# Low parts of the gate and up weights: written by an accumulating DMA instead of VectorE

## The chip, the cores and the metric

One core of a Trainium2 chip runs the kernel. The metric is the device time of one execution in microseconds, the median of several runs. The engines are called PE (TensorE, with PEld for its weight loads), DVE (VectorE), ACT (ScalarE), POOL (GpSimd) and SP (SyncE), as the profile calls them.

## The reference

A trunk of two layers on 512 tokens of 1024 features, in float32. Each layer mixes a state-space branch and a windowed attention branch, and ends in a gated feed-forward block of 2816 hidden features, which is where the change lies:

```python
    u = rms_norm(h, norm_ffn[layer])
    gate, up = jnp.split(u @ w_gate_up[layer], 2, axis=-1)
    h = h + (jax.nn.silu(gate) * up) @ w_down[layer]
```

## The kernel before

**Products in three parts.** A weight product is made in the float32r format, which carries fewer bits than float32. So each operand is split into a high part (its value in float32r) and a low part (the rest), and each block of the contraction takes three matmuls: high times high, high times low of the activations, low of the weights times high (`split3`, line 245). In the trace the weights are `hi` and `lo`, the normalised activations `nh` and `nl`, or `uh` and `ul` where the tokens' norm factors are still missing.

**The stream of weights.** All weights pass through one list of chunks, in the order of use (lines 495 to 510). A gate or up chunk (`w_gu`) holds one tile of 128 output features: 128 partitions of 8 x 128 values, 512 KB. Three stages handle it. `w_load` (line 197) has SP's queue load it into one of 3 `raw` buffers. `w_split` (line 221) writes `hi` with ACT, which converts `raw` to float32r, and then `lo` with DVE, which subtracts `hi` from `raw`. `hi` and `lo` have 4 buffers each. `proj` (line 335) runs the 24 matmuls of a tile.

**How far ahead.** `w_ahead` (line 231) splits chunks up to a number and keeps loads up to 3 chunks beyond. `proj` calls it at its start and half-way, so that while chunk c runs, `hi` of chunk c + 3 is written; its buffers are those of chunk c - 1. A `raw` buffer is loaded again once the split has read it.

**The start of gate and up.** `proj_first` (line 368) runs the first three tiles together, a block of the contraction at a time, since the last block of their input comes late. Meanwhile DVE and ACT work out the norm's factors and the normalised input (`Norm.finish`, line 478: `un`, `nh`, `nl`). The fourth tile also takes the input without factors (`NRAW` = 4); DVE multiplies the products of these four by the factors afterwards (`nu`). Tiles 4 to 43 take `nh` and `nl`. Since the first three tiles hold three pairs of buffers until their end, the split of chunk 4 has to wait for the end of the first tiles.

**Evacuation.** A gate tile leaves its PSUM bank `acc` by a tanh on ACT (`ft`) and a product on DVE (`fg`); an up tile by a product on DVE (`fu`), a conversion on ACT (`fh`) and a subtraction on DVE (`fl`), lines 1133 to 1155. These are the inputs of the down products.

**The order.** Each engine carries out its instructions in the order in which the program issues them. That order comes from a rough account of time in the program (`Clock`, line 70): work beside the weight products is issued when by this account its operands are ready (`poll`, line 294). POOL adds and multiplies in the branches and has nothing to do in the feed-forward block. All lines of compute instructions read L66 in the profile, since a helper issues them; loads from SP read L141.

Of the kernel before, what the change touches and what calls it, by code (L numbers as in the profile page):

```python
# [16 lines left out]
T = 512  # L17
# [26 lines left out]

# columns of the packed constants
C_ID, C_TRI, C_ONE, C_M0, C_M12, C_COS, C_SIN = 0, 128, 256, 384, 512, 768, 1280
NRES = 768
NCONST = 1792
# columns of one layer's packed vectors
V_NM, V_NF, V_CW, V_CB, V_DS, V_SN, V_DTB, V_AL = 0, 8, 16, 112, 136, 152, 168, 200  # L50
# [4 lines left out]
class Engine:  # L55
    """Passes an engine's calls on and keeps the time at which it is through with them."""

# [12 lines left out]
class Clock:  # L70
    """A rough account of when each tile is ready, by which the order of issue is chosen: work that
    hangs on other engines is put between the weight products when its operands are there."""

# [59 lines left out]
def trunk_kernel(ctx: ExitStack, tc: tile.TileContext, xT, consts, vecs, w_in, w_v0, w_v, w_ssd, w_attn,  # L133
# [45 lines left out]
    def take(n):  # L179
        """Waits until n of the side work's banks are free, and takes them."""  # L180
        while room[0] < n:
            yield
        room[0] -= n
# [7 lines left out]

# [1 line left out]
    chunks = []  # L193
    raws, parts_, freed = {}, {}, {}
    state = {"load": 0, "split": 0, "use": 0}
# [8 lines left out]
    def w_halves(i, part):  # L204
        """The first chunks by halves of the contraction: loaded (part 0, 1), split (2, 3)."""
        nk, f = chunks[i].shape[1], chunks[i].shape[2]
        s = slice(part % 2 * (nk // 2), (part % 2 + 1) * (nk // 2))
        if part == 0:
            raws[i] = wpool.tile([P, nk, f], F32, tag="raw", bufs=RAW_BUFS, name=f"raw{i}")
        if part < 2:  # L210
            load(raws[i][:, s, :], chunks[i][:, s, :])
            return
        if part == 2:
            parts_[i] = [wpool.tile([P, nk, f], F32R, tag=x, bufs=HL_BUFS, name=f"{x}{i}") for x in ("hi", "lo")]
        hi, lo = parts_[i]
        sca.activation(out=hi[:, s, :], in_=raws[i][:, s, :], func=AF.Copy)
        dve.tensor_tensor(out=lo[:, s, :], in0=raws[i][:, s, :], in1=hi[:, s, :].bitcast(F32), op=ALU.subtract)
        if part == 3:
            del raws[i]

    def w_split(i):
        raw = raws.pop(i)
        nk, f = raw.shape[1], raw.shape[2]
        hi = wpool.tile([P, nk, f], F32R, tag="hi", bufs=HL_BUFS, name=f"hi{i}")
        lo = wpool.tile([P, nk, f], F32R, tag="lo", bufs=HL_BUFS, name=f"lo{i}")
        sca.activation(out=hi, in_=raw, func=AF.Copy)
        dve.tensor_tensor(out=lo, in0=raw, in1=hi.bitcast(F32), op=ALU.subtract)
        parts_[i] = (hi, lo)
        freed[i] = clock.ready[Clock.key(lo)]
# [22 lines left out]

# [1 line left out]
    class Task:  # L254
# [11 lines left out]
    def arrived(t):  # L266
        """Waits for a load."""
        while clock.ready[Clock.key(t)] > clock.now["pe"]:
            yield
# [24 lines left out]
    def poll():  # L294
        """Runs the next stage of whatever has its operands by now."""
        for name in active:
# [27 lines left out]
    def drain(ready):  # L324
        """Runs the side work until ready(): nothing else is left to do before that."""
        while not ready():
            clock.now["pe"] += 0.3
            poll()
# [6 lines left out]
    def proj(act, nk, ev, nchunks=1):  # L335
        """One tile of 128 output features: nk blocks of the contraction, in nchunks chunks."""
        ps = acc_room()
# [12 lines left out]
    def proj_tokens(act, nk, ev, pss, nchunks):  # L350
        """256 or more output features with the tokens on partitions, in two banks or four."""
        uh, ul = act
# [15 lines left out]
    def proj_first(n, evs, at=3):  # L368
        """The first tiles after a norm, from its input that lacks the tokens' factors: a block of the
        contraction at a time, as the last one comes late. The factors are worked out meanwhile."""  # L370
        norm = isinstance(n, Norm)
# [20 lines left out]

# [1 line left out]
    def rsqrt_small(vv, n):  # L394
        """1/sqrt of a small tile, by Newton steps from the exponent's halving."""
        y = small("nr_y", n, 2)
# [10 lines left out]
    def norm_sums(sq, cs=range(4)):  # L407
        """Sums over features of a tile of squares, a column for each 128 tokens."""
        ps = bank()
# [9 lines left out]
    def norm_rows(y):  # L419
        """The tokens' factors as a row, on every partition."""  # L420
        ps = bank()
# [11 lines left out]
    class Norm:  # L433
        """u = h * w, in two parts; the tokens' factors are applied to the products."""

# [35 lines left out]
        def finish(self, fs):  # L471
            """The normalised input in two parts."""
            def low(u, hi, lo):
# [13 lines left out]

# [1 line left out]
    for l in range(DEPTH):  # L489
# [14 lines left out]
        for f in range(KD):  # L504
            chunks.append(w_out[l, f])
        for f in range(2 * KF):
            chunks.append(w_gu[l, f])
        for f in range(KD):
# [30 lines left out]
    for l in range(DEPTH):  # L539
        L = {}  # L540

        def normed(ps, raw):
            """A product, times the tokens' factors if its input lacked them."""
            if not raw:
# [4 lines left out]

        # -- dt, its running sums and decays --  # L550
        def ev_dt(pss):
            """The columns behind the first heads' V: dt's, with tokens on partitions."""
            tmp = slot(nm="dtt")
# [58 lines left out]

        # -- SSD: convolution and gate where the products come out --
        def ev_conv(g, what, ps, raw=False):
# [34 lines left out]
        def ssd_tasks(g, l, L):  # L649
# [6 lines left out]
            def hd(t, c):  # L656
                """A small tile's values of this group's heads in chunk c, for each of 64 columns."""
                return t[:, c * 32 + 8 * g:c * 32 + 8 * g + 8].unsqueeze(2).to_broadcast([P, 8, 64])
# [4 lines left out]
            def prep():  # L663
                """B C^T of each chunk, x dt and B with tokens on partitions, the states between chunks."""
                while "acr" not in L:
# [65 lines left out]
            def decays():  # L731
                """C B^T times exp(a_cum[l] - a_cum[s]), a head at a time."""
                while "acr" not in L:
# [86 lines left out]

        # -- attention --
        def ev_attn(hd, what, ps):
# [17 lines left out]
        def ev_v(hp, pss):  # L840
            """V of two heads with tokens on partitions, and again with tokens 4 j + a in tile a."""
            vn, vp = [slot(nm="vn"), slot(nm="vn")], [slot(nm="vp"), slot(nm="vp")]
# [20 lines left out]
        def attn_chain(hd, l, L):  # L863
# [22 lines left out]

            # pattern 0: tile i's queries on the keys of tiles i - 1 and i, packed as (0, 1), (2, 3)
            yield from take(2)
# [15 lines left out]
            for i in range(4):  # L904
                b, o, n = where[i]
                sca.activation(out=p0[b][:, o:o + n * P], in_=p0[b][:, o:o + n * P], func=AF.Exp,
                               scale=SCALE, bias=nb[:, i:i + 1], accum_out=st[:, 4 + i:5 + i])
            # patterns 1 and 2: tokens 4 j + a of tile a
            yield from take(2)
# [14 lines left out]
            for a in range(4):  # L924
                o = (a % 2) * 256
                sca.activation(out=p1[a // 2][:, o:o + 256], in_=p1[a // 2][:, o:o + 256], func=AF.Exp,
                               scale=SCALE, bias=nb[:, 4 + a:5 + a], accum_out=st[:, 12 + a:13 + a])
            # transposes of pattern 0's weights: block (i, cur) at i, block (i, prev) at i - 1
            yield from take(2)
# [93 lines left out]

        # -- branch outputs, gates --
        def parts_of(x, to):
            """A tile in two parts, at the end of the lists to."""
            hi, lo = slot(F32R, nm="ah"), slot(F32R, nm="al")
# [80 lines left out]

        # -- output projection, residual --
        nf = Norm(v(l, V_NF, 8))  # L1110
# [17 lines left out]

        # -- feed-forward --
        hid = ([], [])  # L1130
# [37 lines left out]

    # -- the last tile by halves of the tokens, the final norm behind each --
    ws = [w_next(0) for _ in range(3)]  # L1170
# [45 lines left out]
def in_order(l):  # L1216
    """The order of a layer's products up to the output projection: columns of the input projection
    ("in"), groups of the SSD branch ("a"), tiles of the attention branch ("b")."""
    def S(g):
# [6 lines left out]
    def mix(*lists):  # L1226
        """The lists' items in turn, each list spread over the whole."""
        n = [(i + 0.5) / len(x) for x in lists for i in range(len(x))]
# [19 lines left out]
def _columns():  # L1248
    """w_in's columns by tile: (z | x | B | C | dt | q | k | v | g_ssd | g_attn) in the kernel's numbering."""
    z0, x0, b0, c0, dt0 = 0, 2048, 4096, 4608, 5120  # L1250
# [89 lines left out]
```

## Time and profile before

| what | value |
|---|---|
| median of 3 runs | 2398.57 us (2398.03 to 2398.86) |
| span of the profiled execution | 2397.4 us |
| PE, DVE, ACT, POOL busy | 2370.2, 1309.6, 982.4, 162.4 us |
| mean granted clock of PE | 0.997 |
| gate and up chunks, in both layers | 88 of 512 KB |
| matmul of 512 columns, mean | 389 ns in the gate and up stage |
| high part of a chunk, ACT | 1.05 us |
| low part of a chunk, DVE | 1.23 us |

The profiled execution's span runs from its first to its last instruction; its own time with what lies around that is not given, so the span is set beside the median of the runs. Matmuls overlap in the pipeline: one takes 389 ns, but they start some 227 ns apart. In a timeline row stand the start, the duration, the engine, the instruction with its output and input, and in brackets the idle time of the engine before it and what ended that.

### The profile page before, as it was taken

The page shows a single profiled execution, that of the slowest core. Times are in us where ns is not written, and L with a number is a line of the kernel's source. Part 1 is how long each engine was busy: PE and PEld are TensorE (multiplying, and loading weights), DVE is VectorE, ACT ScalarE, POOL GpSimd, SP SyncE. Part 2 cuts the span into 40 slices and gives each one's busy share as a digit, 9 for nine tenths or more (in the row PEclk, how much of TensorE's full clock was granted, in tenths as well). Part 3 has the DMA queues.
Part 4 walks back from the last instruction along what each step waited for, and adds up shares of the span by engine and source line. Part 5 has one row for each costly group of instructions (what it writes and reads, how often), then busy time and mean ns, then how long its engine had stood idle before and what let it go on. Part 6 is the DMA issues. An engine that isn't in the chain of part 4 may idle for free.

```text
span 2397.4 us, 30515 instructions
## 1 busy us (share of the span) xinstructions
PE 2370.2 (99%) x11830; PEld 1982.2 (83%) x11830; DVE 1309.6 (55%) x2099; ACT 982.4 (41%) x1697; POOL 162.4 (7%) x132
## 2 busy tenths in 40 slices
PE   8999999999999999999999999999999999999998
PEld 6878888888888888888888887888888888888887
DVE  7566656565555564443375647566545545644333
ACT  5454545554532332222245445364635323322222
POOL 0011111011000000000001101011110000000000
PEclk9999999999999999999999999999999999999999
DMA  4534435343333322233334344353433333322331
GB/s 154 171 91 137 133 92 153 95 147 111 102 104 105 131 97 99 95 99 106 117 112 147 98 144 127 95 151 114 124 104 113 113 105 110 106 97 97 94 98 64
DMA packets 100704, 272.83 MB, mean 114 GB/s; under 512 B 13584, under 2 KB 20368, under 8 KB 100560
## 3 DMA queue, kind: packets, MB, share of 16 engines
q1 hardware_dynamic: 100560, 270.89, 35.6%
q8 instruction: 93, 1.52, 0.3%
q14 instruction: 51, 0.42, 0.1%
HBM read 251.64 MB, written 10.81 MB: 109 GB/s over the span
## 4 chain that ended last, share of the span: by engine, by line
PE 95%; DVE 2%; DMA 1%; ACT 1%; SPq 0%; issue 0%; POOL 0%; DVEq 0%; POOLq 0%
PE acc L66 84%; PE ps L66 10%; DMA R<-acr 1%; DVE lo L66 1%; SPq L141 0%; DVE cacc L66 0%; DVE z L66 0%; DMA h<-xT 0%; DVE h L66 0%; DMA k<-rp 0%; ACT hi L66 0%; DMA raw<-w_in 0%; DVE un L66 0%; ACT uh L66 0%; ACT sq L66 0%
## 5 line engine op out<-in xcount | busy, mean ns | idle before, releaser
L66 PE MATMUL acc<-nh,hi 128*128 128x512 f32 x1984 | 791.3, 399 | 2.1 <-DVE nu L66 2.1
L66 DVE TENSOR_TENSOR lo<-raw,hi 128x1024 fp32r<-128x1024 f32 (+2 forms) x397 | 490.1, 1238 | 536.3 <-ACT hi L66 531.7
L66 PE MATMUL acc<-nh,lo 128*128 128x512 f32 x1984 | 774.0, 390 | 0.0
L66 PE MATMUL acc<-nl,hi 128*128 128x512 f32 x1984 | 773.3, 390 | 0.0
L66 ACT ACTIVATE hi<-raw 128x1024 fp32r<-128x1024 f32 (+2 forms) x397 | 409.0, 1032 | 234.4 <-PE acc L66 133.9
L66 PEld LDWEIGHTS acc<-nh,hi 128*128 128x128 f32 x1984 | 373.3, 188 | 79.0 <-issue 5.9
L66 PEld LDWEIGHTS acc<-nh,lo 128*128 128x128 f32 x1984 | 372.8, 188 | 78.9
L66 PEld LDWEIGHTS acc<-nl,hi 128*128 128x128 f32 x1984 | 373.4, 188 | 77.2 <-issue 3.4
L66 PE MATMUL acc<-ah,hi 128*128 128x512 f32 x384 | 151.0, 393 | 0.0
L66 PE MATMUL acc<-ah,lo 128*128 128x512 f32 x384 | 149.6, 389 | 0.0
L66 PE MATMUL acc<-al,hi 128*128 128x512 f32 x384 | 149.4, 389 | 0.0
L66 PE MATMUL acc<-fh,hi 128*128 128x512 f32 (+1 forms) x374 | 141.1, 377 | 0.5 <-DVE h L66 0.5
L66 PE MATMUL acc<-fl,hi 128*128 128x512 f32 (+1 forms) x374 | 140.8, 376 | 0.0
L66 PE MATMUL acc<-fh,lo 128*128 128x512 f32 (+1 forms) x374 | 140.8, 376 | 0.0
L66 ACT ACTIVATE fh<-fu 128x512 fp32r<-128x512 f32 x44 | 27.8, 632 | 190.2 <-DVE fu L66 190.2
L66 DVE SCALAR_TENSOR_TENSOR cacc<-acc,vec,cacc 128x511 f32<-128x511 f32 (+2 forms) x120 | 89.4, 747 | 16.4 <-ACT cacc L66 13.6
L66 POOL TENSOR_TENSOR rs<-rs,sin 128x512 f32<-128x512 f32 x16 | 27.6, 1728 | 997.0 <-DVE rs L66 997.0
L66 ACT ACTIVATE p<-p,nb 128x256 f32<-128x256 f32 (+1 forms) x128 | 61.8, 484 | 70.2 <-DVE nb L66 70.1
L66 ACT ACTIVATE R<-R,acum 128x128 f32<-128x128 f32 x256 | 81.1, 388 | 16.2 <-DMA R<-acr 16.2
L66 PEld LDWEIGHTS acc<-ah,lo 128*128 128x128 f32 x384 | 72.1, 188 | 15.3
L66 PEld LDWEIGHTS acc<-al,hi 128*128 128x128 f32 x384 | 72.1, 188 | 14.7
L66 PEld LDWEIGHTS acc<-ah,hi 128*128 128x128 f32 x384 | 72.1, 188 | 14.4
(172 smaller groups left out, 2958.2 us busy)
## 6 DMA issues: line engine op xcount, KB each, us to landing
raw<-w_in SPq DMA_DIRECT2D x173, 512.0 KB
raw<-w_gu SPq DMA_DIRECT2D x88, 512.0 KB
R<-acr SPq DMA_DIRECT2D x64, 256.0 KB
raw<-w_ssd SPq DMA_DIRECT2D x32, 512.0 KB
raw<-w_dn SPq DMA_DIRECT2D x32, 512.0 KB
E<-acr SPq DMA_DIRECT2D x64, 128.0 KB
r<-fd SPq DMA_DIRECT2D x32, 256.0 KB
raw<-w_attn SPq DMA_DIRECT2D x16, 512.0 KB
```

The costliest lines, as they stand in the source:

```text
L66: return f(*a, **kw)
```

## The change

For the chunks of the gate and up products from the fifth one of each layer on (40 per layer, 80 in all) the low part is made in another way. ACT writes the high part as before, and then writes into `lo` the chunk once more with its sign turned, converted to float32r in the same way: the negated high part. Then a DMA from POOL's queue reads the chunk from memory a second time and adds it to `lo`. What is left is the chunk less its high part, as before. DVE has no part in it. The `raw` buffer is free when ACT has read it twice. The account of time hears of ACT's second instruction and not of the DMA.

```diff
     chunks = []
+    by_dma = set()
...
         sca.activation(out=hi, in_=raw, func=AF.Copy)
+        if i in by_dma:
+            sca.activation(out=lo, in_=raw, func=AF.Copy, scale=-1.0)
+            freed[i] = clock.ready[Clock.key(lo)]
+            nc.gpsimd.dma_start(lo, chunks[i], accum_op=ALU.add)
+            parts_[i] = (hi, lo)
+            return
         dve.tensor_tensor(out=lo, in0=raw, in1=hi.bitcast(F32), op=ALU.subtract)
         parts_[i] = (hi, lo)
         freed[i] = clock.ready[Clock.key(lo)]
...
         for f in range(2 * KF):
+            if f >= NRAW:
+                by_dma.add(len(chunks))
             chunks.append(w_gu[l, f])
```

The rest of the diff takes comments and docstrings out. PE's and SP's instructions stand in the same order in both kernels. On ACT the 80 new instructions stand right behind the high parts; on DVE the 80 subtractions are gone; POOL gets 80 DMAs in a row of 40 for each layer.

ACT's order before, at the start of gate and up in layer 0. `hi_7263`, `hi_7303` and `hi_7321` are the high parts of chunks 4, 5 and 6; the numbers of tiles differ a little between the two programs.

```order
L66 ACTIVATE nh_7228<-un_7227 128x512
L66 ACTIVATE hi_7263<-raw_7096 128x1024
L66 ACTIVATE ft_7270<-nu_7267 128x512
L66 ACTIVATE ft_7280<-nu_7277 128x512
L66 ACTIVATE nh_7283<-un_7282 128x512
L66 ACTIVATE nh_7288<-un_7287 128x512
L66 ACTIVATE nh_7294<-un_7293 128x512
L66 ACTIVATE hi_7303<-raw_7122 128x1024
L66 ACTIVATE hi_7321<-raw_7261 128x1024
```

The same place after, where chunks 4, 5 and 6 are `hi_7263`, `hi_7304` and `hi_7323`:

```order
L66 ACTIVATE nh_7228<-un_7227 128x512
L66 ACTIVATE hi_7263<-raw_7096 128x1024
L66 ACTIVATE lo_7264<-raw_7096 128x1024
L66 ACTIVATE ft_7271<-nu_7268 128x512
L66 ACTIVATE ft_7281<-nu_7278 128x512
L66 ACTIVATE nh_7284<-un_7283 128x512
L66 ACTIVATE nh_7289<-un_7288 128x512
L66 ACTIVATE nh_7295<-un_7294 128x512
L66 ACTIVATE hi_7304<-raw_7122 128x1024
L66 ACTIVATE lo_7305<-raw_7122 128x1024
L66 ACTIVATE hi_7323<-raw_7261 128x1024
L66 ACTIVATE lo_7324<-raw_7261 128x1024
```

Each negated high part stands right behind its high part, ahead of the evacuation (`ft`) and of the normalised input (`nh`) that followed the high part before.

POOL's order after, at the same place. The first two rows are its last work in the attention branch of layer 0:

```order
L66 TENSOR_TENSOR p_6211<-p_6145 128x256
L66 TENSOR_TENSOR p_6211<-p_6146 128x256
L231 DMA lo_7264<-w_gu 128x1024
L231 DMA lo_7305<-w_gu 128x1024
L231 DMA lo_7324<-w_gu 128x1024
```

Before, POOL's next row there is its first work of layer 1; the 40 DMAs of the layer have come in between, each waiting for its negated high part.

## The prediction

> **What bounds the kernel now.** I read the page first, then who TensorE (PE) waits for, then the chain of waits and the stages of the changed products.
>
> The page of the kernel before:
>
> ```profile
> span 2397.4 us, 30515 instructions
> ...
> PE 2370.2 (99%) x11830; PEld 1982.2 (83%) x11830; DVE 1309.6 (55%) x2099; ACT 982.4 (41%) x1697; POOL 162.4 (7%) x132
> ...
> PEclk9999999999999999999999999999999999999999
> ...
> PE 95%; DVE 2%; DMA 1%; ACT 1%; SPq 0%; issue 0%; POOL 0%; DVEq 0%; POOLq 0%
> ```
>
> PE is busy all the time at full clock and is 95% of the chain that ended last. All that PE waited for between 45 and 2370 us (total, times, longest), and the chain's longest piece in layer 0:
>
> ```profile
> PE ps L66 <- DVE H L66: 3.3, 2, 1.7
> PE ps L66 <- DVE xdt L66: 1.3, 2, 0.9
> PE ps L66 <- ACT tpp L66: 0.6, 1, 0.6
> ```
>
> ```profile
> 850.59 355.01 PE acc L66 x1566
> ```
>
> None of these waits is for a weight chunk. The 355 us piece covers the whole gate and up stage of layer 0 without a gap. The stages themselves (stretch, its length, busy time of PE, PEld, DVE, ACT, POOL, then clock, DMA share, GB/s):
>
> ```profile
> 871.00:1220.00 349.00, 349.00 (x1547) 289.17 (x1546) 145.99 (x176) 101.04 (x129) 0.00 (x0) 1.00 0.31 103
> 2054.00:2270.00 216.00, 216.00 (x955) 178.85 (x954) 93.17 (x106) 64.82 (x84) 0.00 (x0) 1.00 0.29 100
> ```
>
> So DVE is 42% busy there, ACT 29%, POOL idle, the DMA engines 30%: PE alone is full. Time can be lost here, hardly won.
>
> **The change, part by part.** *Removed:* 80 subtractions on DVE. *Added:* 80 negations on ACT, 80 DMAs from POOL's queue. PE's and SP's orders stay as they were, row for row. In the steady stage the rows are
>
> ```profile
> 900.32 0.60 ACT L66 ACTIVATE ft<-acc 128x512 f32<-128x512 f32 x1 [3.13 <-PE acc L66]
> 900.81 1.05 ACT L66 ACTIVATE hi<-raw 128x1024 fp32r<-128x1024 f32 x1
> 906.48 0.63 ACT L66 ACTIVATE fh<-fu 128x512 fp32r<-128x512 f32 x1 [4.62 <-DVE fu L66]
> 907.02 1.04 ACT L66 ACTIVATE hi<-raw 128x1024 fp32r<-128x1024 f32 x1
> 911.20 0.60 ACT L66 ACTIVATE ft<-acc 128x512 f32<-128x512 f32 x1 [3.13 <-PE acc L66]
> ```
>
> ```profile
> 901.89 1.23 DVE L66 TENSOR_TENSOR lo<-raw,hi 128x1024 fp32r<-128x1024 f32 x1 [0.26 <-ACT hi L66]
> ```
>
> Two chunks take 911.20 - 900.32 = 10.88 us, so one takes 5.44 us. *DVE* loses 80 x 1.23 = 98 us of work that nobody on the path waited for: worth 0. *ACT* gains 80 x 1.05 = 84 us; two such passes on 5.44 us beside 0.6 us of other work leave it about half idle: cost 0 by its busy time. What counts is when lo is there.
>
> *Steady chunks.* The hi of chunk c + 4 is written when chunk c has ended (900.2) and frees its buffers. With the negation behind it ACT is through at about 902.8 (odd chunks: 909.0, from an end at 905.6). PE needs that lo three chunks after the end of c, 16.3 us, at about 916.6 (922.0). The DMA has 13 us. As long as it takes less than that, and the DMA engines keep up with 5.44 us a chunk, it costs 0. If the cover goes, each us beyond 13 us is lost on PE.
>
> *The first changed chunk of each layer* has no such lead: its hi waits for buffers and nh work at the end of the first three tiles. Layer 0, ACT, then the weight load by which PE first needs lo of chunk 4:
>
> ```profile
> 856.63 0.63 ACT L66 ACTIVATE nh<-un 128x512 fp32r<-128x512 f32 x1 [0.63 <-DVE un L66]
> 857.16 1.04 ACT L66 ACTIVATE hi<-raw 128x1024 fp32r<-128x1024 f32 x1
> ...
> 864.55 1.99 ACT L66 ACTIVATE hi<-raw 128x1024 fp32r<-128x1024 f32 x2
> ```
>
> ```profile
> 862.27 0.19 PEld L66 LDWEIGHTS acc<-nh,lo 128*128 128x128 f32 x1
> ```
>
> Two such passes back to back take 1.99 us, so hi and negation end at 857.16 + 1.99 = 859.15, and the DMA has 862.27 - 859.15 = 3.1 us. Layer 1 is the same:
>
> ```profile
> 2040.66 1.04 ACT L66 ACTIVATE hi<-raw 128x1024 fp32r<-128x1024 f32 x1
> ```
>
> ```profile
> L66 PEld LDWEIGHTS acc<-nh,lo x80: 187/188/188, 2045.8 to 2099.5; 128*128 128x128 f32 x80
> ```
>
> 2045.8 - 2042.65 = 3.1 us. Before, DVE had this lo done at 859.5, 2.8 us early:
>
> ```profile
> 858.24 1.23 DVE L66 TENSOR_TENSOR lo<-raw,hi 128x1024 fp32r<-128x1024 f32 x1 [0.26 <-ACT hi L66]
> 859.38 1.88 DVE L66 TENSOR_TENSOR nu<-acc,rstd 128x512 f32<-128x512 f32 x3
> ```
>
> Chunk 5 follows: without lo, DVE's nu comes 1.14 us earlier, and with it ACT's second hi (864.55 becomes 863.4). Its negation ends at 865.4, its lo is needed at 862.27 + 5.44 = 867.7: 2.3 us. Chunk 6, its two passes right behind (865.4 + 2.0), has 867.7 + 5.44 - 867.4 = 5.7 us, to which PE's own lateness by then is added.
>
> *S, the time from the negation's end until lo is usable.* No accumulating DMA and none from POOL's queue is in this trace. The nearest rows: from issue to the waiting ACT for a plain load of the same 512 KB (in the chain); and the share of all 16 engines that one such load took in the stretch from 903.1 to 908.5 us:
>
> ```profile
> 16.26 3.59 DMA raw<-w_in
> ```
>
> ```profile
> q1 hardware_dynamic: 144, 0.52, 29.5%
> ```
>
> 0.295 x 5.4 = 1.59 us of transfer, so 2.0 us of the 3.59 us are fixed. The add must read both the chunk and lo: two reads, 2 x 1.59. And the moment the negation ends, SP sends the next raw load, which waited for the same buffer, onto the same engines:
>
> ```profile
> 859.49 0.33 SPq L141 DMA_DIRECT2D raw<-w_gu  x1
> ```
>
> That adds up to 1.59 us. S = 2.0 + 3.18 + 1.59 = 6.8 us, my value. Low end: 3.59 us, if read and add cost nothing and nothing collides. High end: three passes (read, read, write) 2.0 + 4.77 + 1.59 = 8.4 us, plus POOL's preparation, for which no row exists; its nearest is its 1.73 us operation, so 10.1 us:
>
> ```profile
> L66 POOL TENSOR_TENSOR rs<-rs,sin 128x512 f32<-128x512 f32 x16 | 27.6, 1728 | 997.0 <-DVE rs L66 997.0
> ```
>
> The Trainium skill, "DMA: Bandwidth & Descriptors", section "Anatomy of one DMA", gives a plain DMA from GpSimd's queue as 2.0 us plus its bytes at 436 GB/s; an estimate by it, with a second read and no collision, is 4.4 us and a time of 2402.8 us. No run here shows it, and it knows no add.
>
> *What a stall costs beyond itself.* Early in layer 0 PE waited 2.11 us, and its clock fell (last windows: clock is the first of the last three numbers):
>
> ```profile
> 37.34 0.76 PE L66 MATMUL acc<-nh,hi 128*128 128x512 f32 x1 [2.11 <-DVE nu L66]
> ```
>
> ```profile
> 36.00:38.00 2.00, 0.66 (x2) 0.60 (x3) 2.00 (x4) 0.00 (x0) 0.00 (x0) 0.81 0.23 36
> 38.00:40.00 2.00, 2.00 (x6) 1.55 (x5) 1.97 (x4) 0.89 (x2) 0.00 (x0) 0.50 0.30 112
> 40.00:42.00 2.00, 2.00 (x9) 1.63 (x8) 1.90 (x4) 1.25 (x3) 0.00 (x0) 0.84 0.00 0
> 42.00:44.00 2.00, 2.00 (x11) 1.65 (x10) 1.88 (x3) 2.00 (x3) 0.00 (x0) 1.00 0.00 0
> ```
>
> At half clock for 2 x (0.19 + 0.50 + 0.16) / 0.5 = 3.4 us, which loses 1.7 us. I charge that for any stall of 2.1 us or more. The Trainium skill, "TensorE: Matmul & The Clock Gate", Part 1, has the clock fall only after an idle window of about 3.4 us; the trace's 2.11 us stall disagrees, so the row decides. By the page, the stall of the sum below would just be long enough, and a shorter one would cost no clock.
>
> *Sum per layer.* Chunk 4: idle S - 3.1 = 3.7 us, clock 1.7 us, together 5.4 us. Chunk 5 would be late by S - 2.3 = 4.5 us, but PE is 5.4 us late by then: nothing more. Two layers: 10.8 us. The span goes from 2397.4 to 2408.2 us; the median of the runs, 2398.57 us, lies 1.17 us above the profiled span, so the prediction is 2409.4 us. With S from 4.9 us to 10.1 us (a stall of 1.8 to 7.0 us) this case runs from 2403.8 (lag S - 2.3, no clock loss) to 2416 us (2 x (7.0 + 1.7)).
>
> **The rivals.**
>
> *Not slower: the cover holds at the start.* Place: chunk 4 of each layer. At S = 3.59 us the lag is S - 2.3 = 1.3 us a layer, 2.6 us in all: 2401.2 us. A measurement of this kernel tells some 0.2%, 4.8 us, from no change, so this decides up to S = 4.7 us. For it: the load row and idle DMA engines. Against it: two reads and the raw load that starts together with it.
>
> *Slower by far: the DMA engines become the bound.* A chunk's raw load and its add must fit 5.44 us: the add may use 5.44 - 1.59 = 3.85 us of the engines. Two reads (3.18 us) fit, three passes (4.77 us) don't: 0.92 us x 80 chunks = 74 us, 2472 us. For it: nothing in this trace shows how fast the engines add. Against it: the engines read and write at the same time in a plain load, so two reads are likelier than three passes.
>
> *Faster: PE's pace.* If DVE's traffic held PE up, half the DVE work gone would speed the products. 80 x 24 = 1920 matmuls; from 2.5 ns each the gain shows, 2393.8 us. PE's steps without DVE (the first two rows, nine steps) and during lo (the last two, five steps):
>
> ```profile
> 898.76 0.39 PE L66 MATMUL acc<-nh,hi 128*128 128x512 f32 x1
> ...
> 900.80 0.39 PE L66 MATMUL acc<-nh,hi 128*128 128x512 f32 x1
> ...
> 901.93 0.39 PE L66 MATMUL acc<-nh,lo 128*128 128x512 f32 x1
> ...
> 903.07 0.39 PE L66 MATMUL acc<-nl,hi 128*128 128x512 f32 x1
> ```
>
> 227 ns and 228 ns: DVE hardly matters.
>
> **How the numbers follow.** Start-up stall 0.58; cover holds 0.22; DMA bound or a DMA beyond 13 us 0.17; faster pace 0.03. So slower 0.75, same 0.22, faster 0.03. The range takes the first two cases, from 2398.5 (no cost at all) to 2425 us (some 4 us a layer beyond the high end, for POOL's unseen preparation); the DMA-bound case and the faster one, 0.20, are left out.
>
> **What would show it.** Right: in the changed profile PE waits at two places only, for lo of the fifth w_gu chunk of each layer (and perhaps the sixth), 2 to 7 us long, with the clock at 0.5 for some 3 us behind it; from there PE is gapless and DMA share is about 0.9. Wrong: PE waits at every chunk (the DMA bound, or more than 13 us from negation to use); no wait at all (S under 3.1 us); or a loss in another stage.

## The result and the profile after

The changed kernel takes 2413.28 us in the median (3 runs, 2411.11 to 2414.32), the kernel before 2398.57 us: 14.7 us more, a ratio of 1.006 with a 95% interval of 1.004 to 1.008. Slower, as forecast, by somewhat more than the 10.8 us of the sum. The profiled execution's span is 2409.3 us, 11.9 us above that of before.

The page after: span, busy times, clock, and the new queue, which carries the adds:

```profile
span 2409.3 us, 30647 instructions
...
PE 2373.1 (98%) x11830; PEld 1982.2 (82%) x11830; DVE 1212.3 (50%) x2019; ACT 1058.1 (44%) x1777; POOL 231.8 (10%) x212
...
PEclk9999999999999999999999999999999999999999
...
q0 software_dynamic: 11520, 41.95, 9.9%
...
lo<-w_gu POOLq DMA_DIRECT2D x80, 512.0 KB, 7.8
```

DVE has 97 us less to do, ACT 76 us more, and an add takes 7.8 us in the median from issue to landing. What PE waited for in the whole execution, longest in total first:

```profile
PE acc L66 <- DMA lo<-w_gu: 10.5, 3, 4.8
PE acc L66 <- ACT hi L66: 6.5, 1, 6.5
PE ps L66 <- DVE H L66: 3.3, 2, 1.7
```

The second row is the wait for the first weights at the program's start, which the kernel before has too. The first row is new, and it stands for three waits out of 80 adds. They are the first of each layer and the second of layer 0. ACT, POOL and PE there, layer 0 (ACT: the fifth chunk's `hi`, its negated high part, and the negation of chunk 5; POOL: the issue of the fifth chunk's add; PE: its first product with that `lo`, and its wait for the `lo` of chunk 5):

```profile
854.99 1.04 ACT L66 ACTIVATE hi<-raw 128x1024 fp32r<-128x1024 f32 x1
855.94 1.05 ACT L66 ACTIVATE lo<-raw 128x1024 fp32r<-128x1024 f32 x1
...
861.84 1.04 ACT L66 ACTIVATE lo<-raw 128x1024 fp32r<-128x1024 f32 x1
```

```profile
857.31 1.01 POOL L231 DMA_DIRECT2D lo<-w_gu  x1 [151.81 <-DVE nu L66]
```

```profile
864.99 0.80 PE L66 MATMUL acc<-nh,lo 128*128 128x512 f32 x1 [4.51 <-DMA lo<-w_gu]
...
873.44 0.50 PE L66 MATMUL acc<-nh,lo 128*128 128x512 f32 x1 [1.22 <-DMA lo<-w_gu]
```

The profile names DVE's `nu` as what POOL waited for. But POOL's rows begin 0.29 to 0.32 us after the negation's end at each of the first five adds of a layer, so it is the negation that lets the add go. In layer 1 there is one wait:

```profile
2055.77 0.62 PE L66 MATMUL acc<-nh,lo 128*128 128x512 f32 x1 [4.81 <-DMA lo<-w_gu]
```

The clock behind the long waits (stretch, length, busy PE, PEld, DVE, ACT, POOL, then clock, DMA share, GB/s):

```profile
864.00:866.00 2.00, 1.01 (x2) 0.84 (x3) 1.61 (x3) 2.00 (x3) 0.93 (x2) 0.69 0.79 252
866.00:868.00 2.00, 2.00 (x6) 1.62 (x5) 0.02 (x1) 1.19 (x2) 0.52 (x1) 0.50 0.70 119
868.00:870.00 2.00, 2.00 (x9) 1.57 (x9) 0.00 (x0) 0.00 (x0) 0.34 (x1) 0.96 0.97 254
```

```profile
2056.00:2058.00 2.00, 2.00 (x6) 1.52 (x6) 0.50 (x1) 1.67 (x2) 0.45 (x2) 0.50 0.79 137
2058.00:2060.00 2.00, 2.00 (x7) 1.59 (x6) 0.00 (x0) 0.00 (x0) 0.82 (x1) 0.65 0.99 225
```

Layer 0 loses 2 x (0.31 + 0.50 + 0.04) = 1.7 us to the clock, layer 1 2 x (0.50 + 0.35) = 1.7 us. Behind the second wait of layer 0 the gate and up stage is gapless again, in the chain and by its window:

```profile
873.44 337.84 PE acc L66 x1489
```

```profile
880.00:1080.00 200.00, 200.00 (x884) 165.62 (x883) 40.52 (x58) 90.51 (x109) 30.18 (x35) 1.00 0.83 188
```

The waits (4.5 + 1.2 + 4.8) and the clock (3.4) make 13.9 us. (Idle time counts from the end of the last matmul, 0.39 us after its start, where the next would have started 0.23 us after it: some 0.16 us more a wait.) The profiled spans differ by 11.9 us because this execution was 2.2 us ahead before anything changed: PE began the fifth chunk at 859.9 us, before at 862.0. The start is where the two profiles differ, in code that is the same. The first 45 us before and after (clock 0.92 and 1.00):

```profile
0.00:45.00 45.00, 34.56 (x137) 27.44 (x138) 33.47 (x61) 25.29 (x40) 0.20 (x4) 0.92 0.49 159
```

```profile
0.00:45.00 45.00, 35.16 (x152) 27.65 (x152) 34.03 (x62) 26.37 (x41) 0.20 (x4) 1.00 0.49 169
```

So single executions vary by a few us; the medians, 14.7 us apart, are the better match for the 13.9 us of waits and clock and the 0.5 us beside them.

The two traces settle it, since both hold the same 11830 matmuls in the same order. Set side by side, matmul for matmul, PE loses 7.9 us between the start of the fifth chunk and 880 us, and 7.1 us at the same place of layer 1: 15.0 us in all. The rest of the difference is the 2.2 us of the first 45 us and 0.9 us between 1300 and 1500 us, both in favour of the changed kernel and in code that is the same.

### The profile page after: what moved, and what is told of

It is laid out like the page before. It is cut to its first block, busy times and chain, and to the rows that moved or that the text cites. A ratio compares the mean times of both kernels' runs of the same rounds, so it can differ in the third digit from the quotient of the medians.

```text
span 2409.3 us, 30647 instructions
## 1 busy us (share of the span) xinstructions
PE 2373.1 (98%) x11830; PEld 1982.2 (82%) x11830; DVE 1212.3 (50%) x2019; ACT 1058.1 (44%) x1777; POOL 231.8 (10%) x212
## 4 chain that ended last, share of the span: by engine, by line
PE 87%; issue 9%; DVE 2%; DMA 1%; ACT 1%; SPq 0%; POOL 0%; DVEq 0%; ACTq 0%; POOLq 0%
PE acc L66 77%; PE ps L66 10%; DMA lo<-w_gu 1%; DVE lo L66 1%; ACT hi L66 0%; DVE h L66 0%; DVE cacc L66 0%; DMA h<-xT 0%; ACT sq L66 0%; ACT uh L66 0%; DVE un L66 0%; DVE sq L66 0%; DVE ul L66 0%; DVE nl L66 0%; DVE nr_t L66 0%
## 5 line engine op out<-in xcount | busy, mean ns | idle before, releaser
L66 PE MATMUL acc<-nh,lo 128*128 128x512 f32 x1984 | 775.5, 391 | 10.6 <-DMA lo<-w_gu 10.5
L66 DVE TENSOR_TENSOR lo<-raw,hi 128x1024 fp32r<-128x1024 f32 (+4 forms) x317 | 392.1, 1241 | 505.6 <-ACT hi L66 502.7
L231 POOL DMA_DIRECT2D lo<-w_gu x80 | 69.2, 865 | 655.3 <-ACT lo L66 339.9
L66 DVE SCALAR_TENSOR_TENSOR fu<-acc,fg 128x512 f32<-128x512 f32 x40 | 27.7, 692 | 161.8 <-PE acc L66 161.8
L66 DVE SCALAR_TENSOR_TENSOR fg<-ft,acc 128x512 f32<-128x512 f32 x40 | 27.5, 687 | 161.8 <-ACT ft L66 161.8
```

What stands on the lines that cost most here:

```text
L66: return f(*a, **kw)
L231: nc.gpsimd.dma_start(lo, chunks[i], accum_op=ALU.add)
```

## The experiments

The theory: nothing but the first chunks of each layer costs time, where the lead from the negation to PE's first use (3.1 us) is shorter than the add; PE waits, and a long wait halves its clock for a while. The rivals: each add costs something, by the load on the DMA engines or by ACT's second pass. In the runs with the experiments the kernel before took 2398.3 to 2398.9 us.

**Adds from the thirteenth chunk on.**

```diff
-            if f >= NRAW:
+            if f >= 12:
                 by_dma.add(len(chunks))
```

> The add by DMA from the thirteenth gate and up chunk of each layer on (32 instead of 40 chunks a layer); the first twelve keep the subtraction on DVE. Theory (the loss is PE's wait for the first changed chunks, whose lead is shorter than the add takes): from the thirteenth chunk the lead is about 13 us, the add takes about 8, so PE waits nowhere for lo and the time is that of the kernel before, 2398.6 us within 2 us, although four fifths of the adds are left. Rival (the adds cost something each, by DMA load or by ACT's second pass): 64 of 80 adds remain, so 64/80 of the 14.7 us remain, about 2410 us.

Measured: 2398.55 us, ratio 0.9997 (0.9988 to 1.0006). PE's longest waits hold no lo of a w_gu chunk, with 64 adds left at about the same duration:

```profile
PE acc L66 <- ACT hi L66: 7.1, 1, 7.1
PE ps L66 <- DVE H L66: 3.3, 2, 1.7
```

```profile
lo<-w_gu POOLq DMA_DIRECT2D x64, 512.0 KB, 7.6
```

With that lead the adds themselves cost nothing; a cost per add is ruled out.

**The add for the fifth chunk alone.**

```diff
-            if f >= NRAW:
+            if f == NRAW:
                 by_dma.add(len(chunks))
```

> The add by DMA for the fifth gate and up chunk of each layer alone, two adds in all. Theory: the wait at that chunk stays, some 4 to 5 us a layer plus 1.7 us at half clock behind it, 11 to 13 us in all; the second wait of 1.2 us in layer 0 goes with the other adds: 2409 to 2412 us. Rival (a cost per add): 2 of 80 adds, 0.4 us, 2399 us.

Measured: 2410.40 us, ratio 1.0048 (1.0036 to 1.0061). Two adds of 80 bring back 11.7 of the 14.7 us:

```profile
PE acc L66 <- DMA lo<-w_gu: 8.1, 2, 4.7
```

```profile
lo<-w_gu POOLq DMA_DIRECT2D x2, 512.0 KB, 7.2
```

The waits are 3.36 and 4.71 us, and both are followed by products at half clock. 8.1 + 2 x 1.7 = 11.5 us. The theory holds, and the 1.2 us of chunk 5 is gone with its add.

**Adds from the seventh chunk on.**

```diff
-            if f >= NRAW:
+            if f >= 6:
                 by_dma.add(len(chunks))
```

> The add by DMA from the seventh chunk of each layer on; chunks 4 and 5 keep the subtraction on DVE. Theory: by the rows of before the seventh chunk's negation ends some 5.7 us ahead of its first use; with an add of 8 us PE waits about 2.3 us a layer, and loses 1.7 us more a layer if a wait of that length still halves the clock: plus 4.6 us without the clock's part, 2403 us; plus 8 us with it, 2407 us. Rival (a cost per add): 76 of 80 adds, 2412 us.

Measured: 2405.62 us, ratio 1.0028 (1.0017 to 1.0039), between the two values. One wait a layer:

```profile
875.56 0.50 PE L66 MATMUL acc<-nh,lo 128*128 128x512 f32 x1 [1.98 <-DMA lo<-w_gu]
```

```profile
2061.03 0.50 PE L66 MATMUL acc<-nh,lo 128*128 128x512 f32 x1 [2.45 <-DMA lo<-w_gu]
2061.64 0.63 PE L66 MATMUL acc<-nl,hi 128*128 128x512 f32 x1
```

The waits are as long as the lead of before foretold (about 2.3 us). Behind 1.98 us the clock stayed whole, behind 2.45 us it halved (products of 0.63 us); what decides this stands in the last section. With one clock loss the sum is 4.4 + 1.7 = 6.1 us, measured 6.9 us.

**ACT's second pass without the DMA.**

```diff
             sca.activation(out=lo, in_=raw, func=AF.Copy, scale=-1.0)
             freed[i] = clock.ready[Clock.key(lo)]
-            nc.gpsimd.dma_start(lo, chunks[i], accum_op=ALU.add)
             parts_[i] = (hi, lo)
```

> ACT's second pass stays, the DMA is left out: lo holds the negated high part, so the low part of these weights is not computed. Theory: ACT's pass costs nothing on the path and lo is there 2 us ahead of its first use, so 2398.6 us within 2 us. Rival (ACT's 84 us more of work delay the evacuations or the high parts, and are part of the loss): over 2403 us.

Measured: 2398.68 us, ratio 1.0000 (0.9991 to 1.0009). ACT's 80 more passes and DVE's 80 fewer come to nothing together; one without the other was not run.

Two more runs take the add's duration apart.

**A converting copy in place of the add.**

```diff
-            nc.gpsimd.dma_start(lo, chunks[i], accum_op=ALU.add)
+            nc.gpsimd.dma_start(lo, chunks[i])
```

> As the changed kernel, but the DMA from POOL's queue only copies the chunk into lo, converted to float32r, without adding: one read less, and lo is not the low part, so that part of the computation is not done. The adds take 7.8 us in the median from issue to landing. If the second read is a good part of that (1.6 us by itself, more beside a raw load), the copy lands after about 6 us, PE waits about 3 us at the fifth chunk and the time is about 2407 us. If the path by POOL's queue is slow by itself whatever it moves, landing stays above 7.3 us and the time about 2412 us.

Measured: 2403.84 us, ratio 1.0021 (1.0012 to 1.0030). The queue's share, the duration and PE's wait:

```profile
q0 software_dynamic: 11520, 41.95, 4.8%
...
lo<-w_gu POOLq DMA_DIRECT2D x80, 512.0 KB, 4.6
```

```profile
PE acc L66 <- DMA lo<-w_gu: 3.9, 3, 2.1
```

A copy occupies the engines for 0.048 x 2402.3 / 80 = 1.44 us, an add for 0.099 x 2409.3 / 80 = 2.98 us, twice that, and lands 3.2 us later. So POOL's queue alone does not make the add long; what it does beyond a copy makes 3.2 us of it. The factor of two speaks for the second read, but the read and the adding were not taken apart. The waits came out shorter than expected.

**The next raw load held back from the fifth chunk's add.** (Adds for the fifth chunk alone; last_raw holds that chunk's raw buffer.)

```diff
         raw = raws.pop(i)
+        last_raw[0] = raw
...
             n.finish(range(NEARLY, KD))
+            if first + NFIRST + 1 in by_dma:
+                sca.activation(out=warm, in_=last_raw[0][:, 0, 0:1], func=AF.Copy)
...
-            if f >= NRAW:
+            if f == NRAW:
```

> The add for the fifth chunk alone, as in the second experiment, but ACT reads one column of that chunk's raw buffer once more behind the last nh, about 4 us later, so that SP's next raw load starts 4 us after the add and not beside it. If the collision with the raw load is part of the add's duration: landing falls from 6.5 and 7.9 us to 5 to 6 us, the two waits from 8.1 us to about 5 us in all, 2407 us. If not: landing stays, 2410.4 us.

Measured: 2406.26 us, ratio 1.0029 (1.0017 to 1.0042), 4.1 us below the same kernel without the hold. Landing, and the waits:

```profile
lo<-w_gu POOLq DMA_DIRECT2D x2, 512.0 KB, 5.5
```

```profile
865.34 0.50 PE L66 MATMUL acc<-nh,lo 128*128 128x512 f32 x1 [2.46 <-DMA lo<-w_gu]
```

```profile
2052.68 0.50 PE L66 MATMUL acc<-nh,lo 128*128 128x512 f32 x1 [2.19 <-DMA lo<-w_gu]
```

Nearly alone the add takes 5.6 us in layer 0 and 5.3 us in layer 1; beside the raw load it took 6.5 and 7.9 us. So the collision costs 0.9 and 2.5 us, 1.7 us in the mean. The clock stayed whole here behind 2.46 and 2.19 us in the profiled execution. The two waits, 4.7 us, are less than the 8 us by which the median lies above before. Set against the trace of before matmul for matmul, this execution, 6.9 us longer in its span, loses 5.3 us at the two adds. Another 1.3 us goes in the branches of layer 1, in code that is the same: there the clock was halved from 1478.0 to 1481.4 us behind a wait of 1.66 us, which the kernel before has too and got over at full clock. The other five executions were not profiled.

**How near the DMA engines are to being the bound.** First each changed chunk loaded twice (adds from the thirteenth chunk on):

```diff
         load(raw, ap, freed.get(i - RAW_BUFS, 0.0))
+        if i in by_dma:
+            load(raw, ap)
...
-            if f >= NRAW:
+            if f >= 12:
```

> Adds from the thirteenth chunk on, as in the first experiment, and each of these chunks is loaded into its raw buffer twice, one load after the other: 1.6 us more of the DMA engines a chunk. The adds and the single load take 82% of the engines in that stage, 4.5 of 5.44 us; with the second load 6.1 us. If the engines then are the bound, PE waits at nearly every one of the 64 chunks, by about 0.6 us in the mean: 2435 to 2445 us. If the bound is elsewhere (the share counts time in which more would fit): 2399 us.

Measured: 2482.01 us, ratio 1.0346 (1.0327 to 1.0365), 83.7 us slower and so above either value. But the share did not fill up: 0.85 in the stretch from 930 to 1080 us, where ACT waited for the raw loads most of all, and SP's queue, which issues them, for a load to land:

```profile
930.00:1080.00 150.00, 128.34 (x521) 102.89 (x520) 22.11 (x32) 50.87 (x61) 17.52 (x21) 0.93 0.85 218
```

```profile
ACT hi L66 <- DMA raw<-w_gu: 82.6, 19, 8.1
```

```profile
SPq L141 <- DMA raw<-w_gu: 127.4, 20, 8.4
```

SP issues the second load into a buffer only when the first has landed, and waits for that 127 of the 150 us, 6.4 us a chunk, longer than the 5.44 us that PE takes for one. So the two loads were a chain of their own, and this run can't tell. A copy that nobody waits for was tried instead:

```diff
         load(raw, ap, freed.get(i - RAW_BUFS, 0.0))
+        if i in by_dma:
+            spare = dpool.tile([P, nk, f], F32, tag="spare", bufs=2, name=f"sp{i}")
+            nc.sync.dma_start(spare, ap)
...
-            if f >= NRAW:
+            if f >= 12:
```

> Adds from the thirteenth chunk on, as in the first experiment, and behind each of their raw loads SP sends one more DMA that copies the same 512 KB to a spare buffer in DRAM that nothing reads. Unlike the double load it lengthens no chain of waits by itself, it only takes some 1.6 us of the DMA engines a chunk. If the engines are the bound (4.5 + 1.6 = 6.1 us against 5.44 us a chunk): at least 0.7 us x 64 = 42 us more, about 2440 us. If the double load was slow for its chain of two loads alone: within 10 us of 2398.6 us.

Measured: 2398.63 us, ratio 0.9999 (0.9989 to 1.0008). The stretch from 930 to 1070 us, first without the copy (the first experiment), then with it, and the adds' duration with it:

```profile
930.00:1070.00 140.00, 140.00 (x619) 115.95 (x618) 29.18 (x41) 63.37 (x76) 20.70 (x24) 1.00 0.86 190
```

```profile
930.00:1070.00 140.00, 140.00 (x619) 115.94 (x618) 27.49 (x39) 62.98 (x77) 21.61 (x25) 1.00 1.01 279
```

```profile
lo<-w_gu POOLq DMA_DIRECT2D x64, 512.0 KB, 9.4
```

The adds land after 9.4 us, still within the 13 us of lead, and PE waits for none. So the loss of the double load came from its chain, and the changed kernel, at 0.83, is not bound by its DMA engines. That a share above 1 would cost nothing had not been expected. It also shows that the share is no measure of how full the engines are: at 0.86 they moved 190 GB/s, at 1.01 they moved 279, so at 0.86 there was room for nearly half as much again. (The copy goes to DRAM, not to SBUF; a second stream into SBUF was not tried without a chain.)

**Adds for the down products too** (from the thirteenth gate and up chunk on, and all 48 down chunks).

```diff
-            if f >= NRAW:
+            if f >= 12:
...
             for k0, k1 in ((0, 8), (8, 16), (16, 22)):
+                by_dma.add(len(chunks))
                 chunks.append(w_dn[l, f, :, k0:k1, :])
```

> Adds from the thirteenth gate and up chunk on, and for all chunks of the down products too: 112 adds in all. Theory (only the lead counts): in the down products the lead is about 13 us as well for full chunks and less by 1.4 us where a chunk of six blocks lies in it, against an add of 8 us, so no wait and 2398.6 us within 2 us. Rival (the norm behind the residual or the last tile, which hang on ACT, get later by ACT's second passes): 2401 us or more.

Measured: 2398.41 us, ratio 0.9997 (0.9988 to 1.0006). 112 adds with a long lead cost nothing.

**The add from the raw buffer.**

```diff
-            nc.gpsimd.dma_start(lo, chunks[i], accum_op=ALU.add)
+            nc.gpsimd.dma_start(lo, raw, accum_op=ALU.add)
```

> As the changed kernel with all 80 adds, but the DMA adds the chunk from its raw buffer instead of reading it from DRAM again. The raw buffer then stays taken until the add has landed, so no raw load starts beside the add of the same chunk. If the collision with the raw load costs as in the sixth experiment: landing at the fifth chunk 5.5 us or a little more, waits of 2.2 to 2.5 us a layer, 2406 us or less. If reading SBUF on both sides is slower than DRAM and SBUF: landing at 7 us or more, 2411 us or more.

Measured: 2404.51 us, ratio 1.0024 (1.0014 to 1.0034): 5.7 us above its own runs of before, where the changed kernel stood 14.7 us above. Landing and the waits of layer 0:

```profile
lo<-raw POOLq DMA_DIRECT2D x80, 512.0 KB, 5.9
```

```profile
862.61 0.50 PE L66 MATMUL acc<-nh,lo 128*128 128x512 f32 x1 [1.52 <-DMA lo<-raw]
869.84 0.50 PE L66 MATMUL acc<-nh,lo 128*128 128x512 f32 x1 [1.47 <-DMA lo<-raw]
```

Landing is shorter, the waits are under 2 us and split over two chunks, and the clock is kept there. For the fifth chunk's add both parts can be read off: it lands after 4.7 us in layer 0 and 4.5 us in layer 1, where the add from DRAM took 5.6 and 5.3 us with the raw load held back, and 6.5 and 7.9 us beside it. So without the collision the add from the raw buffer is still 0.8 to 0.9 us shorter; the nearer source is the plain reading of that, from one execution of each.

No version beat the kernel before. Those with a long lead equal it.

## Why the prediction was right, step by step

- *DVE's work is worth 0, ACT's costs 0.* Shown for the two together by ACT's pass without the DMA: 2398.68 us.
- *Steady chunks are covered.* Shown by the adds from the thirteenth chunk on and by the gapless stage. The duration there is 7.6 us against 13 us of lead.
- *The fifth chunk's lead is 3.1 us and PE waits there.* Shown by two adds that bring back 11.7 us. The idle time was put at 3.7 us a layer and is 4.5 and 4.8 us. The term that was too small is S, 6.8 us: from the negation's end (856.99) to PE's weights it was 8.0 us, in layer 1 8.3 us. That and chunk 5 make the loss 7.9 and 7.1 us a layer where the sum had 5.4.
- *S's parts.* Two reads: confirmed in size, 2.98 us of engine time against 3.18. An add alone, put at 2.0 + 3.18 = 5.2 us, takes 5.5 us. The collision, put at up to 1.59 us, is the part that was too small: in the changed kernel the fifth chunk's adds landed after 7.6 and 8.0 us, 2.1 and 2.5 us later than alone. Left out were the 0.3 us from ACT's end to POOL's row (856.99 to 857.31).
- *Chunk 5 adds nothing.* Failed in layer 0, where PE waited 1.2 us more: "nothing more" took the same S for chunk 5, but from its negation's end (862.88) to PE's product (873.44) it was 10.6 us. The add itself took 10.2 us to land, and the next two, issued 1.9 and 4.3 us behind it, 12.1 and 12.9 us; that adds close behind each other slow each other is likely, and was not tried. In layer 1 the same add landed after 9.5 us and PE lost 0.2 us to it: the step held there, by little.
- *1.7 us of clock per layer.* Right in size, 1.7 us in both. The condition, any stall of 2.1 us or more, is wrong as a rule, and that the row it was read from showed a fall was luck: the same wait in the changed kernel's profile, 2.10 us, left the clock whole. So did waits of 2.11 us (the copy, layer 1), 2.19 and 2.46 us (the held load); one of 2.45 us didn't. All waits for an add of 3.36 us and more halved it. The Trainium skill, "TensorE: Matmul & The Clock Gate", Part 1, with its idle window of about 3.4 us, fits the long waits, and the wait of 2.45 us contradicts it.
- *The rivals.* The cover did not hold. The DMA engines were not the bound, not even with a copy of every chunk on top. PE's pace did not change with DVE's load: nothing was won where no wait stood.
- *DMA share of about 0.9 afterwards*: it is 0.83.

## What to carry to other kernels

A step that is moved to a path of longer latency has to be judged at its first use, not by its mean: here 77 of 80 adds had 13 us of lead or enough of it (one of them lost 0.2 us), and three cost all the rest. Where a stage starts with less lead than the path needs, leave the first few steps on the fast engine: from the thirteenth chunk on the change is free, and still takes 64 x 1.23 = 79 us of work from DVE. That only pays if DVE is waited for somewhere, which in this kernel it hardly is.

## What the runs showed of the hardware

- An accumulating DMA of 512 KB from POOL's queue took 5.5 us alone, 7.2 to 7.8 us in the median beside plain loads of the same size, up to 12.9 us behind other adds, and 9.4 us with a copy of each chunk on top; added from SBUF, alone, 4.6 us. A converting copy on the same queue took 4.6 us in the median. The engine time of an add, 2.98 us, is about twice that of the copy, 1.44 us.
- With the DMA engines' share at 1.01 nothing was lost as long as the adds landed within their lead.
- Whether a wait of 2 to 2.5 us halves PE's clock is not fixed by its length: 2.45 us did, 2.46 us didn't. The traces show what decides. In each of the 12 profiled executions the granted clock changes only at times that lie whole multiples of 3.41 us apart (before: 23.59, 27.01, 37.25, 40.66, 2389.03 us). What counts among products of 512 columns is how long PE is idle within one such stretch. The wait that the prediction took its rule from, 2.11 us before, and the same wait after, 2.10 us, on the stretches of their own executions:

```profile
33.82:37.23 3.41, 1.41 (x7) 0.83 (x5) 3.06 (x5) 1.51 (x2) 0.00 (x0) 1.00 0.00 0
37.23:40.65 3.42, 3.31 (x8) 2.67 (x9) 3.39 (x6) 1.26 (x2) 0.00 (x0) 0.50 0.31 86
```

```profile
31.90:35.31 3.41, 1.90 (x9) 1.24 (x7) 3.06 (x5) 1.58 (x2) 0.00 (x0) 1.00 0.00 0
35.31:38.73 3.42, 2.83 (x12) 2.36 (x13) 3.38 (x6) 1.06 (x2) 0.00 (x0) 1.00 0.32 86
```

Before, one stretch holds 2.00 us of idle time, and the clock is halved in the next; after, the wait falls on two stretches, 1.51 and 0.59 us, and the clock stays whole. Likewise the 2.45 us lay in one stretch, and the 2.46 us on two (0.70 and 1.76 us). In the gate and up stages of all these executions a stretch at full clock with 1.92 us or more of idle time was followed by half clock, and none with 1.90 us or less was. Elsewhere, among narrower products, 1.0 to 1.7 us was enough in some executions and not in others, which is not explained. By these figures a wait of 3.9 us or more halves the clock wherever it falls (an estimate: half of it, 1.95 us, lies in one stretch). So the charge for the two long waits was sound, and the rule behind it was not. A lost stretch cost 1.7 us.
